# Scaling of the query rows on ScalarE instead of GpSimd, and the 32-wide products of the block inverse issued in turn for both halves

## The chip, the core and the metric

The kernel runs on one core of one Trainium2 chip. A core has TensorE (PE in the profile, matrix products; its weight loads are shown as PEld), VectorE (DVE), ScalarE (ACT), GpSimd (POOL) and SyncE (SP, which here issues most of the DMA transfers). Each engine works off its own list of instructions in order and waits for others by semaphores. The metric is the device time of one execution in microseconds (us), and the median of the runs counts.

## What is computed

The reference is one block of a hybrid sequence model, with 512 positions of width 1024 in f32: a SwiGLU feed-forward network, a mixer and a second feed-forward network, each with a residual sum and an adaptive norm. The mixer has two groups of four heads side by side, a gated delta rule and a latent attention (MLA). Cut to the parts that the change touches:

```python
# gated delta rule: a unit lower triangular system per chunk and head
M = A + jnp.eye(CHUNK, dtype=A.dtype)
W = lax.linalg.triangular_solve(M, rhs, left_side=True, lower=True, unit_diagonal=True)
...
# latent attention: the RMS norm of each head's query, plain and rotary part
q_nope = _rms(q_nope, qkn_q_nope) * scale
q_rope = _rope(_rms(q_rope, qkn_q_rope), cos[:, :, None], sin[:, :, None]) * scale
...
mixed = jnp.concatenate([o_a, o_b], axis=-1)
return mixed @ w_out
```

## The kernel before

The 512 positions are four token blocks of 128. Dense products are made in units of 128 output columns: a weight load from DRAM (tile `wr`, 512 KB, issued by SyncE at line 118), a cast to a high part on ScalarE (`wh`, line 193), the rest on VectorE (`wl`, line 198), and three matmuls of 512 columns per step of 128 (lines 266, 267 and 268) into an accumulator `pa`. There are three such PSUM buffers, and five of the other kind, `pb`, for everything small.

The code is written as generators, one per chain of small work: the delta rule, its block inverse, the preparation of queries and keys, the attention of one token block. The mixer's dense units call a step function that advances these chains at fixed rates, so that small work goes in between the 512-column matmuls of `w_in` (four groups of four units). A scheduler of the tile framework then settles the order of each engine's instructions before the run: tiles are handed out from pools, and an instruction that writes a buffer waits for the last reader of the tile that had it. A changed instruction in one chain can therefore move instructions of others, weight loads among them. After that the order is fixed.

*Queries.* `prep_q` (line 1730) takes eight tiles `upo` (four token blocks, two pairs of heads), each with two heads of 128 plain and 64 rotary columns. It works out 16 reciprocal norms for the plain part (`rqn`) and 16 for the rotary part. VectorE multiplies the rotary columns (`qrx`, by the helper `mul`, line 1206), rotates them (lines 1830 to 1834, result `qro`), and TensorE transposes `qro` at line 1768, copied to `qrT` by ScalarE at line 1770. The plain columns are multiplied in place by GpSimd, eight instructions of 128x256 (lines 1773 to 1776, by `mul`, so that the profile shows line 1206), and TensorE transposes them at line 1725.

*Block inverse.* `inverse` (line 1533) inverts, for one token block `p` and four heads at once, unit triangular blocks of 128 by doubling: the inverses of the 16-wide diagonal blocks come from `base_blocks` (forward substitution on VectorE in `bw` and `bt`, with two passes through DRAM, `a_d` to `ba` at line 1508 and `t_d` to `t` at lines 1526 and 1528), products with masks give those of 32 (lines 1553 and 1559), then of 64 (lines 1569 and 1577), then of 128 (lines 1592 and 1598). The 32-wide products use a 32x32 tile of the array each. There are two halves of the 128 rows, `j` = 0 and 64; for each half there are four products (one per head) and then a copy of the half, on ScalarE at line 1571 (`Y`), or on VectorE at line 1579 (`U`). Four inverses, one per token block, run in turn. A product in f32 issues two matmul instructions.

*Attention.* `attend` multiplies queries and keys (lines 1847 and 1850), takes row maxima on VectorE (`mx`, line 1856), exponentials on ScalarE (line 168, `pr`), transposes (line 1867), copies (`pT`, line 1871), multiplies with the values (line 1877) and copies the result (`ao`, line 1879). `attended` norms it (`on`), transposes it (line 1900) and splits it (`mh`, line 1905, on ScalarE; `ml`, line 1906, on VectorE). In the same stretch ScalarE copies the finished gate units `z` out of their accumulators (line 1921).

Of the kernel before, what the change touches and what calls it, by code (L numbers as in the profile page):

```python
# [14 lines left out]
AF = mybir.ActivationFunctionType  # L15
# [3 lines left out]
P = 128  # L19
# [60 lines left out]
class Block:  # L80
# [1452 lines left out]
    def inverse(self, p):  # L1533

        nc = self.nc
        h4 = lambda x: x.rearrange("p (h d) -> p h d", h=4)
        hs = lambda h: slice(h * P, (h + 1) * P)
        at = self.at[p]

        def flip(src):  # L1540

            t = self.slot(s="T")
            nc.vector.transpose(out=t, in_=src)
            return t

        t = self.slot(s="t0")
        self.mul(t.rearrange("p (h i c) -> p h i c", h=4, i=8),
                 self.t16[:, 4 * p:4 * p + 4, :].unsqueeze(2).to_broadcast([P, 4, 8, 16]),
                 self.dmask.rearrange("p (i c) -> p i c", i=8).unsqueeze(1).to_broadcast([P, 4, 8, 16]))
        u = flip(t)  # L1550
        py = self.aux()
        for h in range(4):
            nc.tensor.matmul(py[:, hs(h)], at[:, hs(h)], t[:, hs(h)], start=True, stop=True)
        y = self.slot(s="Y")
        self.mul(h4(y), h4(py), self.lmask.unsqueeze(1).to_broadcast([P, 4, P]))
        yield
        pz = self.aux()
        for h in range(4):
            nc.tensor.matmul(pz[:, hs(h)], y[:, hs(h)], u[:, hs(h)], start=True, stop=True)
        un = self.slot(s="U")  # L1560
        nc.vector.tensor_tensor(out=un, in0=u, in1=pz, op=ALU.subtract)
        t = flip(un)
        yield

        py, y = self.aux(), self.slot(s="Y")
        for j in (0, 64):
            a, b = slice(j, j + 32), slice(j + 32, j + 64)
            for h in range(4):
                nc.tensor.matmul(py[b, 32 * h:32 * h + 32], at[a, h * P + j + 32:h * P + j + 64],
                                 t[a, h * P + j:h * P + j + 32], start=True, stop=True, tile_position=(j, j + 32))  # L1570
            nc.scalar.copy(y[b, :P], py[b, :P])
        yield
        pz = self.aux()
        for j in (0, 64):
            a, b = slice(j, j + 32), slice(j + 32, j + 64)
            for h in range(4):
                nc.tensor.matmul(pz[a, 32 * h:32 * h + 32], y[b, 32 * h:32 * h + 32],
                                 un[b, h * P + j + 32:h * P + j + 64], start=True, stop=True, tile_position=(j + 32, j))
            nc.vector.tensor_scalar(out=h4(un[a, :])[:, :, j + 32:j + 64],
                                    in0=pz[a, :P].rearrange("p (h c) -> p h c", h=4), scalar1=-1.0, scalar2=None,  # L1580
                                    op0=ALU.mult)
        yield

        a, b = slice(0, 64), slice(64, P)
        pt, t = self.aux(), self.slot(s="T")
        for h in range(4):
            nc.tensor.transpose(pt[a, 64 * h:64 * h + 64], un[a, h * P:h * P + 64], self.ident[a, a])
        nc.scalar.copy(t[a, :256], pt[a, :256])
        yield
        py, y = self.aux(), self.slot(s="Y")  # L1590
        for h in range(4):
            nc.tensor.matmul(py[b, 64 * h:64 * h + 64], at[a, h * P + 64:h * P + P], t[a, 64 * h:64 * h + 64], start=True,
                             stop=True, tile_position=(0, 64))
        nc.scalar.copy(y[b, :256], py[b, :256])
        yield
        pz = self.aux()
        for h in range(4):
            nc.tensor.matmul(pz[a, 64 * h:64 * h + 64], y[b, 64 * h:64 * h + 64], un[b, h * P + 64:h * P + P], start=True,
                             stop=True, tile_position=(64, 0))
        nc.vector.tensor_scalar(out=h4(un[a, :])[:, :, 64:], in0=pz[a, :256].rearrange("p (h c) -> p h c", h=4),  # L1600
                                scalar1=-1.0, scalar2=None, op0=ALU.mult)
        yield
        self.inv[p] = un
# [126 lines left out]
    def prep_q(self, q):  # L1730

        nc = self.nc

        room = self.slot(s="sq3")
        s3, ve = room[:, :48], room[:, 48:80]
        for b in range(NB):
            for g in range(2):
                c = 6 * (2 * b + g)
                s = self.slot(s="aqq")
                nc.scalar.activation(s[:, :384], q[b][g][:, :384], AF.Square)  # L1740
                nc.vector.tensor_reduce(out=s3[:, c:c + 6], in_=s[:, :384].rearrange("p (e d) -> p e d", e=6), axis=AX.X,
                                        op=ALU.add)
            if b % 2:
                yield
        s3 = s3.rearrange("p (q e) -> p q e", e=3)
        nc.vector.tensor_tensor(out=ve[:, :16], in0=s3[:, :, 0], in1=s3[:, :, 1], op=ALU.add)
        nc.vector.tensor_scalar(out=ve[:, :16], in0=ve[:, :16], scalar1=1.0 / 128, scalar2=EPS, op0=ALU.mult, op1=ALU.add)
        nc.vector.tensor_scalar(out=ve[:, 16:], in0=s3[:, :, 2], scalar1=1.0 / 64, scalar2=EPS, op0=ALU.mult, op1=ALU.add)
        r = self.rsqrt(ve, 32, room[:, 80:112], room[:, 112:144])
        rqn, rqr = r[:, :16], r[:, 16:]  # L1750

        qr = []
        for b in range(0, NB, 2):
            x = self.slot(s="qrx").rearrange("p (b h c) -> p b h c", b=2, h=4)
            for e in range(2):
                for g in range(2):
                    qv = q[b + e][g][:, :384].rearrange("p (h d) -> p h d", h=2)[:, :, 128:]
                    c = 4 * (b + e) + 2 * g
                    self.mul(x[:, e, 2 * g:2 * g + 2, :], qv, self.bc(rqr[:, c:c + 2], 2, 64))
            o = self.slot(s="qro")  # L1760
            tb = lambda t: t[:, b:b + 2, :].unsqueeze(2).to_broadcast([P, 2, 4, 64])
            self.rope(o.rearrange("p (b h c) -> p b h c", b=2, h=4), x, tb(self.rope_c["q"]), tb(self.rope_s["q"]))
            qr += [o[:, :256], o[:, 256:]]
            yield
        for g in range(2):
            pt = self.aux()
            for b in range(NB):
                nc.tensor.transpose(pt[:, b * P:(b + 1) * P], qr[b][:, g * P:(g + 1) * P], self.ident)
            t = self.slot(s="qrT")
            nc.scalar.copy(t, pt)  # L1770
            self.qrT.append(t)

        for b in range(NB):
            for g in range(2):
                qv = q[b][g][:, :384].rearrange("p (h d) -> p h d", h=2)[:, :, :128]
                self.mul(qv, qv, self.bc(rqn[:, 4 * b + 2 * g:4 * b + 2 * g + 2], 2), nc.gpsimd)
        yield
        for h in range(4):
            c = (h % 2) * 192
            self.qnT.append(self.head_tiles([q[b][h // 2][:, c:c + P] for b in range(NB)], self.gqn))  # L1780
            yield
# [324 lines left out]
```

## Time and profile before

| | before |
|---|---|
| runs | 1076.95, 1079.23 and 1079.45 us, median 1079.23 |
| the profiled execution | 1077.71 us, span from first to last instruction 1076.0 |
| mean granted clock of TensorE | 0.987 of full |
| busy: PE, DVE, ACT, POOL | 1046.7, 689.4, 445.3, 51.3 us |
| GpSimd's eight scalings (`upo`) | from 490.80, 5.62 us |
| TensorE's wait for `qro` behind them | 2.60 us, up to 497.02 |
| TensorE's longest wait inside the mixer, for `z` | 4.29 us, up to 600.61 |
| 32-wide matmuls, lines 1569 and 1577 | 64 each, 193 ns each, from 622.33 to 641.4 |

A row of a timeline gives the start in us from the span's start, the length, engine, line, operation, what it writes and reads, how many instructions are grouped (x8; their length then runs from the first start to the last end), and in brackets the idle time of the engine just before, with what ended it. A row of waits gives who waited, for whom, the sum, the number and the longest. A row of the windows gives for each engine its busy time and the instructions, then the granted clock, the share of the DMA engines and GB/s. Matmul instructions overlap, so the distance between their starts, not their length, tells the rate.

### The profile page before, as it was taken

The numbers are of one execution on the slowest core, as the hardware profiler recorded it, in microseconds if no ns is written. First come the engines' busy times: TensorE is split into PE (matmuls) and PEld (weight loads), VectorE is DVE, ScalarE is ACT, GpSimd is POOL, SyncE is SP. The second block draws the span as 40 slices with busy tenths as digits, with TensorE's granted clock in tenths as the row PEclk, the third lists the DMA queues.
The fourth block names the chain that finished last, engine by engine and source line by source line (L and its number), as shares of the span: only waits on it lengthen the run. The fifth ranks groups of instructions, "written<-read, shape, count | busy, mean of one in ns | idle before, by whom it ended". The sixth has DMA issues, their size and how long they took to land. (4 is left out here: it accounts for less than half of the span.)

```text
span 1076.0 us, 15659 instructions
## 1 busy us (share of the span) xinstructions
PE 1046.7 (97%) x6183; PEld 899.1 (84%) x6183; DVE 689.4 (64%) x1231; ACT 445.3 (41%) x761; POOL 51.3 (5%) x103
## 2 busy tenths in 40 slices
PE   6999999999999999998999899999999999999998
PEld 5788878788887898887778578988899999999997
DVE  4488983433577445558868644769768787777633
ACT  3342222222222245566575363465534444444322
POOL 1000000000000011102000030220000000000000
PEclk8999999999999999999999898999999999999999
DMA  9989963233698349411203001153432333233222
GB/s 274 277 240 310 301 203 99 81 98 93 199 289 263 95 120 240 113 49 40 79 25 92 26 21 39 40 126 91 129 107 79 118 115 98 83 118 99 67 71 79
DMA packets 203687, 136.85 MB, mean 127 GB/s; under 512 B 13777, under 2 KB 186590, under 8 KB 203614
## 3 DMA queue, kind: packets, MB, share of 16 engines
q1 hardware_dynamic: 202318, 131.14, 41.1%
q0 software_dynamic: 1296, 4.72, 2.4%
q8 instruction: 48, 0.79, 0.3%
q14 instruction: 25, 0.20, 0.1%
HBM read 128.63 MB, written 2.49 MB: 122 GB/s over the span
## 5 line engine op out<-in xcount | busy, mean ns | idle before, releaser
L266 PE MATMUL pa<-hh,wh 128*128 128x512 f32 (+1 forms) x597 | 227.0, 380 | 4.3 <-ACT z L1921 4.3
L268 PE MATMUL pa<-hh,wl 128*128 128x512 f32 (+1 forms) x597 | 225.0, 377 | 2.7 <-DMA wl<-wr 2.7
L267 PE MATMUL pa<-hl,wh 128*128 128x512 f32 (+1 forms) x597 | 224.8, 377 | 0.0
L193 ACT CAST wh<-wr 128x1024 fp32r<-128x1024 f32 (+1 forms) x106 | 108.0, 1019 | 258.3 <-PE pa L267 184.4
L198 DVE TENSOR_TENSOR wl<-wr,wh 128x1024 fp32r<-128x1024 f32 (+1 forms) x97 | 114.4, 1180 | 99.0 <-ACT wh L193 94.5
L266 PE MATMUL pa<-ah,wh 128*128 128x512 f32 (+1 forms) x396 | 145.5, 367 | 0.6 <-DVE xT L873 0.4
L267 PE MATMUL pa<-al,wh 128*128 128x512 f32 (+1 forms) x396 | 144.5, 365 | 0.0
L268 PE MATMUL pa<-ah,wl 128*128 128x512 f32 (+1 forms) x396 | 143.5, 362 | 0.0
L266 PEld LDWEIGHTS pa<-hh,wh 128*128 128x128 f32 x597 | 113.6, 190 | 27.2 <-ACT z L1921 4.7
L268 PEld LDWEIGHTS pa<-hh,wl 128*128 128x128 f32 x597 | 113.5, 190 | 23.1 <-DMA wl<-wr 3.3
L267 PEld LDWEIGHTS pa<-hl,wh 128*128 128x128 f32 x597 | 113.5, 190 | 19.2 <-DVE hl L453 0.4
L268 PEld LDWEIGHTS pa<-ah,wl 128*128 128x128 f32 x396 | 74.8, 189 | 12.0
L266 PEld LDWEIGHTS pa<-ah,wh 128*128 128x128 f32 x396 | 75.2, 190 | 10.4 <-ACT wh L193 1.7
L267 PEld LDWEIGHTS pa<-al,wh 128*128 128x128 f32 x396 | 75.2, 190 | 7.2
L551 DVE SCALAR_TENSOR_TENSOR aa<-ar,sc,aa 128x512 f32<-128x512 f32 x98 | 73.2, 751 | 9.7 <-DMA ar<-in_w_ada 8.5
L846 PE MATMUL pb<-fh,wh 128*128 128x256 f32 x144 | 40.7, 282 | 0.0
L848 PE MATMUL pb<-fh,wl 128*128 128x256 f32 x144 | 40.7, 283 | 0.0
L848 PE MATMUL pb<-hh,wl 128*128 128x256 f32 x144 | 40.7, 283 | 0.0
L847 PE MATMUL pb<-fl,wh 128*128 128x256 f32 x144 | 40.7, 282 | 0.0
L847 PE MATMUL pb<-hl,wh 128*128 128x256 f32 x144 | 40.7, 282 | 0.0
L846 PE MATMUL pb<-hh,wh 128*128 128x256 f32 x144 | 40.6, 282 | 0.0
L873 DVE SCALAR_TENSOR_TENSOR xT<-pa,mod,xT 128x512 f32<-128x512 f32 (+1 forms) x40 | 29.4, 736 | 17.5 <-PE pa L268 17.5
(433 smaller groups left out, 1995.0 us busy)
## 6 DMA issues: line engine op xcount, KB each, us to landing
wr<-in_ffn_w_in SPq DMA_DIRECT2D x82, 512.0 KB, 4.1
ar<-in_w_ada SPq DMA_DIRECT2D x48, 512.0 KB, 5.9
wr<-in_ffn_w_out SPq DMA_DIRECT2D x34, 512.0 KB, 3.4
ar<-in_w_ada SPq DMA_DIRECT2D x48, 256.0 KB, 4.8
wr<-in_w_in SPq DMA_DIRECT2D x21, 512.0 KB, 3.9
wr<-in_ffn_w_out SPq DMA_DIRECT2D x17, 384.0 KB, 3.4
wl<-wr POOLq DMA_DIRECT2D x9, 512.0 KB, 5.6
wr<-in_w_out SPq DMA_DIRECT2D x8, 512.0 KB, 4.8
```

The source lines that it names most:

```text
L193: self.nc.scalar.copy(hi, raw)
L198: self.nc.vector.tensor_tensor(out=lo, in0=raw, in1=hi.bitcast(F32), op=ALU.subtract)
L266: mm(out, wh, xh, start=start, stop=False)
L267: mm(out, wh, xl, start=False, stop=False)
L268: mm(out, wl, xh, start=False, stop=stop)
L551: nc.vector.scalar_tensor_tensor(out=acc, in0=a, scalar=sc, in1=acc, op0=ALU.mult, op1=ALU.add)
L846: mm(out, wh, xh, start=start and k == 0, stop=False, **kw)
L847: mm(out, wh, xl, start=False, stop=False, **kw)
L848: mm(out, wl, xh, start=False, stop=stop and k == 3, **kw)
L873: nc.vector.scalar_tensor_tensor(out=self.xT[t][:, ts], in0=p[:, ts], scalar=gate[:, t:t + 1], in1=self.xT[t][:, ts], op0=ALU.mult, op1=AL ...
```

## The change

The first part replaces GpSimd's eight multiplications of 128x256 by sixteen activations of 128x128 on ScalarE, each with a scale per row. The second turns the two loops of the 32-wide products around: the heads are now the outer loop and the halves the inner one, and the two copies follow when all eight products are issued. Tiles, sizes and numbers of products stay.

```diff
         py, y = self.aux(), self.slot(s="Y")
-        for j in (0, 64):
-            a, b = slice(j, j + 32), slice(j + 32, j + 64)
-            for h in range(4):
+        for h in range(4):
+            for j in (0, 64):
+                a, b = slice(j, j + 32), slice(j + 32, j + 64)
                 nc.tensor.matmul(py[b, 32 * h:32 * h + 32], at[a, h * P + j + 32:h * P + j + 64],
                                  t[a, h * P + j:h * P + j + 32], start=True, stop=True, tile_position=(j, j + 32))
+        for j in (0, 64):
+            b = slice(j + 32, j + 64)
             nc.scalar.copy(y[b, :P], py[b, :P])
         yield
         pz = self.aux()
-        for j in (0, 64):
-            a, b = slice(j, j + 32), slice(j + 32, j + 64)
-            for h in range(4):
+        for h in range(4):
+            for j in (0, 64):
+                a, b = slice(j, j + 32), slice(j + 32, j + 64)
                 nc.tensor.matmul(pz[a, 32 * h:32 * h + 32], y[b, 32 * h:32 * h + 32],
                                  un[b, h * P + j + 32:h * P + j + 64], start=True, stop=True, tile_position=(j + 32, j))
+        for j in (0, 64):
+            a = slice(j, j + 32)
             nc.vector.tensor_scalar(out=h4(un[a, :])[:, :, j + 32:j + 64],
...
         for b in range(NB):
             for g in range(2):
-                qv = q[b][g][:, :384].rearrange("p (h d) -> p h d", h=2)[:, :, :128]
-                self.mul(qv, qv, self.bc(rqn[:, 4 * b + 2 * g:4 * b + 2 * g + 2], 2), nc.gpsimd)
+                for e in range(2):
+                    qv, c = q[b][g][:, 192 * e:192 * e + P], 4 * b + 2 * g + e
+                    nc.scalar.activation(qv, qv, AF.Copy, scale=rqn[:, c:c + 1])
```

In the lists of the new kernel, tiles from about number 4314 on have numbers higher by 8, and lines lie lower: 1770 is 1774, 1847 is 1852, 1850 is 1855, 1877 is 1882, 1900 is 1905, and the new scaling is line 1781.

*The first place: ScalarE at the scaling.* Before, ScalarE goes there from the values (`vn`) over silu of a convolution (`cv`) and the copies of the delta rule's Gram block (`l2q`, `ktk`) to a weight cast (`wh`):

```order
L1320 ACTIVATE vn_4041<-pa_4205,ry_3787 128x256
L168 ACTIVATE cv_4200<-cv_4200 128x512
L1430 ACTIVATE l2q_4269<-pb_4264 128x512
L1433 COPY ktk_4271<-pb_4264 128x512
L193 CAST wh_4625<-wr_4624 128x1024
L1410 ACTIVATE cv_4361<-pa_4224,cwT_808 128x512
```

In the new kernel the scalings stand in between:

```order
L1781 ACTIVATE upo_3832<-upo_3832,sq_4094 128x128 x2
L1781 ACTIVATE upo_3916<-upo_3916,sq_4094 128x128
L168 ACTIVATE cv_4200<-cv_4200 128x512
L1781 ACTIVATE upo_3916<-upo_3916,sq_4094 128x128
L1781 ACTIVATE upo_3850<-upo_3850,sq_4094 128x128 x2
L1781 ACTIVATE upo_3934<-upo_3934,sq_4094 128x128 x2
L1430 ACTIVATE l2q_4269<-pb_4264 128x512
L1433 COPY ktk_4271<-pb_4264 128x512
L1781 ACTIVATE upo_3868<-upo_3868,sq_4094 128x128 x2
L1781 ACTIVATE upo_3952<-upo_3952,sq_4094 128x128 x2
L1781 ACTIVATE upo_3886<-upo_3886,sq_4094 128x128 x2
L1781 ACTIVATE upo_3970<-upo_3970,sq_4094 128x128 x2
```

Eight of the sixteen stand ahead of the copy to `l2q`, eight between that of `ktk` and the cast.

*The second place: TensorE ahead of its wait for `z`.* `pa_5349` is the last gate unit but one, and `pa_5471` (`pa_5479` in the new kernel) the next, which takes a buffer that `z`'s copy frees. Before:

```order
L266 MATMUL pa_5349<-hh_3169,wh_5227 128x512
L1900 MATMUL pb_5182<-ident_92,on_5180 128x128 x4
L1553 MATMUL pb_5197<-t_5193,at_4551 128x128 x4
L1847 MATMUL pb_5204<-nT_4530,nT_4359 128x256
L1847 MATMUL pb_5205<-nT_4543,nT_4384 128x256
L1850 MATMUL pb_5204<-krT_4426,qrT_4298 128x256
L1850 MATMUL pb_5205<-krT_4426,qrT_4298 128x256
L267 MATMUL pa_5349<-hl_3170,wh_5227 128x512
L268 MATMUL pa_5349<-hh_3169,wl_5228 128x512
L266 MATMUL pa_5471<-hh_3155,wh_5344 128x512
```

and in the new kernel:

```order
L266 MATMUL pa_5357<-hh_3169,wh_5235 128x512
L267 MATMUL pa_5357<-hl_3170,wh_5235 128x512
L268 MATMUL pa_5357<-hh_3169,wl_5236 128x512
L1905 MATMUL pb_5190<-ident_92,on_5188 128x128 x4
L1553 MATMUL pb_5205<-t_5201,at_4559 128x128 x4
L1852 MATMUL pb_5212<-nT_4538,nT_4367 128x256
L1852 MATMUL pb_5213<-nT_4551,nT_4392 128x256
L1855 MATMUL pb_5212<-krT_4434,qrT_4298 128x256
L1855 MATMUL pb_5213<-krT_4434,qrT_4298 128x256
L266 MATMUL pa_5479<-hh_3155,wh_5352 128x512
```

The unit's last two matmuls have moved ahead of the transposes of `on`, the first block product and the attention's products. SyncE's list (weight loads `wr`, the two passes through DRAM) before:

```order
L1504 DMA a_d<-bd_4879 128x16x32
L1508 DMA ba_4897<-a_d 64x16x16 x2
L118 DMA wr_5737<-in_w_out 128x4x256
L118 DMA wr_5882<-in_w_out 128x4x256
L118 DMA wr_6003<-in_w_out 128x4x256
L1526 DMA t_d<-bt_4900 64x256 x2
L1528 DMA t_5138<-t_d 128x16x16
L118 DMA wr_6121<-in_w_out 128x4x256
```

and in the new kernel:

```order
L1504 DMA a_d<-bd_4887 128x16x32
L118 DMA wr_5745<-in_w_out 128x4x256
L1508 DMA ba_4905<-a_d 64x16x16 x2
L118 DMA wr_5890<-in_w_out 128x4x256
L118 DMA wr_6011<-in_w_out 128x4x256
L1526 DMA t_d<-bt_4908 64x256 x2
L118 DMA wr_6129<-in_w_out 128x4x256
L1528 DMA t_5146<-t_d 128x16x16
```

Each of the two reads back from DRAM has got a weight load ahead of it.

*The third place: the 32-wide products on TensorE.* `pb_5440` and `pb_5478` hold the products of the first two inverses; the other rows are gate matmuls and the attention's. Before (a row counts products, each of which issues two matmuls):

```order
L1569 MATMUL pb_5440<-T_5333,at_4551 32x32 x4
L267 MATMUL pa_5471<-hl_3164,wh_5344 128x512
L1877 MATMUL pb_5452<-vn_4038,pT_5406 128x128
...
L1569 MATMUL pb_5478<-T_5363,at_4552 32x32 x4
L268 MATMUL pa_5471<-hh_3163,wl_5345 128x512
L266 MATMUL pa_5471<-hh_3165,wh_5344 128x512
L1569 MATMUL pb_5440<-T_5333,at_4551 32x32 x4
L1877 MATMUL pb_5452<-vn_4038,pT_5432 128x128
...
L1569 MATMUL pb_5478<-T_5363,at_4552 32x32 x4
```

and in the new kernel:

```order
L1569 MATMUL pb_5448<-T_5341,at_4559 32x32 x8
L267 MATMUL pa_5479<-hl_3164,wh_5352 128x512
L1882 MATMUL pb_5460<-vn_4038,pT_5414 128x128
...
L1569 MATMUL pb_5486<-T_5371,at_4560 32x32 x8
L268 MATMUL pa_5479<-hh_3163,wl_5353 128x512
L266 MATMUL pa_5479<-hh_3165,wh_5352 128x512
L267 MATMUL pa_5479<-hl_3166,wh_5352 128x512
```

All eight products of a token block stand in one row, where they were two rows of four with other work between them.

## The prediction

> **What bounds the kernel now.** I read the busy times of the page first, then TensorE's list of waits, then the timelines around the changed lines. Every row is of the one profiled execution, 1077.71 us long with a span of 1076.0; the page opens so:
>
> ```profile
> span 1076.0 us, 15659 instructions
> PE 1046.7 (97%) x6183; PEld 899.1 (84%) x6183; DVE 689.4 (64%) x1231; ACT 445.3 (41%) x761; POOL 51.3 (5%) x103
> ```
>
> TensorE (PE) works in 97% of the span and sets the end: an edit counts by what it takes out of TensorE's row, or by a wait that it shortens there. TensorE's waits, longest in total first:
>
> ```profile
> PE pa L266 <- ACT z L1921: 4.3, 1, 4.3
> ...
> PE pb L1768 <- DVE qro L1834: 2.8, 2, 2.6
> ```
>
> The second row is the end of the chain through the query scaling; the first lies among the instructions that the new order moves. The three stretches follow in the order of the program.
>
> **1. The scaling leaves GpSimd (POOL): -2.6 us.** POOL, VectorE (DVE), then TensorE, start and length ahead of each row:
>
> ```profile
> 490.80 5.62 POOL L1206 TENSOR_TENSOR upo<-upo,sq 128x256 f32<-128x256 f32 x8 [23.95 <-DVE sq L189]
> ```
> ```profile
> 491.25 2.17 DVE L1206 TENSOR_TENSOR qrx<-upo,sq 128x128 f32<-128x128 f32 x4
> ...
> 495.98 0.98 DVE L1834 TENSOR_TENSOR qro<-rt,rt 128x512 f32<-128x512 f32 x1
> ...
> 497.48 0.89 DVE L1206 TENSOR_TENSOR qrx<-upo,sq 128x128 f32<-128x128 f32 x4
> ...
> 499.87 0.69 DVE L1834 TENSOR_TENSOR qro<-rt,rt 128x512 f32<-128x512 f32 x1
> ```
> ```profile
> 494.03 0.39 PE L267 MATMUL pa<-hl,wh 128*128 128x512 f32 x1
> 497.02 0.66 PE L1768 MATMUL pb<-ident,qro 128*128 128x128 f32 x4 [2.60 <-DVE qro L1834]
> ```
>
> VectorE makes qro (the rotated queries) once beside POOL's eight instructions and once after them. Beside them the group takes 496.96 - 491.25 = 5.71 us; after them 500.56 - 497.48 = 3.08 us. Nothing else differs between the two groups, so the scaling slows VectorE by 2.63 us, and TensorE waits 2.60 us for that very product. With POOL still, qro is ready near 491.25 + 3.08 = 494.33, as TensorE gets there (its 512-column matmuls start 0.23 us apart): the wait of 2.60 goes. The waits row has 0.2 at the second group, which I leave.
>
> ScalarE (ACT) gets 16 instructions of 128x128 in place of POOL's 8 of 128x256. No row shows this form from SBUF to SBUF; nearest are two of 128x128 and, for room, what stands next on ScalarE:
>
> ```profile
> L1879 ACT COPY ao<-pb 128x128 f32<-128x128 f32 x16 | 4.1, 266 | 6.3 <-PE pb L1877 6.1
> L1660 ACT ACTIVATE o<-pb,eG 128x128 f32<-128x128 f32 x12 | 3.4, 370 | 4.7 <-PE pb L1658 4.7
> ```
> ```profile
> 499.28 1.05 ACT L193 CAST wh<-wr 128x1024 fp32r<-128x1024 f32 x1 [5.59 <-PE pa L267]
> ```
>
> By those, 16 x 0.27 to 0.37 = 4.3 to 5.9 us, and I take 4.3 (a plain copy with a scale). ScalarE is idle for 5.59 us ahead of that cast, and the eight new instructions that stand ahead of the copies of l2q and ktk delay only VectorE's row sums. So they are costed at nothing; cover gone, the last scaled tiles come up to 0.9 us late for TensorE's transposes of the queries (L1725). Could ScalarE slow VectorE as POOL did? A gain of nothing is the lower bound there, 2.6 the upper. I take the upper: the second group of VectorE ran beside ScalarE's cast and was the fast one.
>
> **2. The long wait at 596 us: -1.5 us.** The new order changes what stands around it on TensorE, ScalarE, VectorE and the queue of SyncE (SP):
>
> ```profile
> 592.42 0.63 PE L1900 MATMUL pb<-ident,on 128*128 128x128 f32 x4 [0.87 <-DVE on L1206]
> 593.03 1.13 PE L1553 MATMUL pb<-t,at 128*128 128x128 f32 x8
> ...
> 594.95 0.70 PE L1850 MATMUL pb<-krT,qrT 64*128 64x256 f32 x4
> 595.59 0.50 PE L267 MATMUL pa<-hl,wh 128*128 128x512 f32 x1
> ...
> 600.61 0.80 PE L266 MATMUL pa<-hh,wh 128*128 128x512 f32 x1 [4.29 <-ACT z L1921]
> ```
> ```profile
> 596.12 1.05 ACT L193 CAST wh<-wr 128x1024 fp32r<-128x1024 f32 x1 [6.80 <-PE pa L267]
> ...
> 598.48 0.47 ACT L168 ACTIVATE pr<-pb,mx 128x256 f32<-128x256 f32 x1
> ...
> 599.97 0.59 ACT L1921 COPY z<-pa 128x512 f32<-128x512 f32 x1
> ```
> ```profile
> 592.19 0.69 DVE L1206 TENSOR_TENSOR t<-t,mk 128x512 f32<-128x512 f32 x1
> ...
> 595.88 0.42 DVE L1856 TENSOR_REDUCE mx<-pb 128x1 f32<-128x256 f32 x1
> ```
> ```profile
> 588.01 0.37 SPq L1528 DMA_DIRECT2D t<-t_d  x1
> 588.47 0.97 SPq L118 DMA_DIRECT2D wr<-in_w_out  x1
> ```
>
> TensorE's matmul at 600.61 writes a buffer that z's copy still reads. z stands on ScalarE behind the cast, which waits 6.80 us for the matmul of line 267 at 595.59, and behind the exponentials. In the new order lines 267 and 268 stand ahead of the transposes of line 1900: the cast is released at about 591.9, and no longer sits between the first row maximum (ready 595.88 + 0.42 = 596.30) and the first exponential (598.48). From there to the end of z's copy are 600.56 - 598.48 = 2.08 us, so z would be done near 598.4.
>
> Against this, on SyncE the two loads of ba, and later the load of t (the inverses of the 16-wide diagonal blocks, which line 1553 multiplies), now each stand behind a 512-KB weight load. The DMA page of 560 to 596 us gives moved GB/s by 0.9-us slices and the landing times:
>
> ```profile
> GB/s 0 0 0 0 79 145 67 0 7 102 205 387 27 0 0 0 0 18 0 0 0 0 0 0 23 269 300 207 311 124 77 0 64 107 258 269 30 0 0 0
> ...
> wr<-in_w_out SPq DMA_DIRECT2D x4, 512.0 KB, 4.8
> ...
> ba<-a_d SPq DMA_DIRECT2D x2, 64.0 KB, 2.7
> ```
>
> At the fastest slice, 387 GB/s, 512 KB pass in 1.35 us (estimate); I take 1.4 for ba and 0.6 more for t, since most of its weight load passes while SyncE still waits for t_d. Both bounds: 0, or the full landing of 4.8. t landed at about 588.01 + 2.7 = 590.7, 1.5 us ahead of VectorE's use of it at 592.19. Landing 2.0 later, it holds line 1553 back by 0.5, and z ends at 598.9 in place of 600.56: 1.7 us less wait, of which I take 1.5, because the second maximum may hold the second exponential. Bounds: the whole 4.29 gained; or t 4.8 later, z at 598.4 + 4.8 - 1.5 = 601.7, and 1.1 us lost.
>
> **3. The products of 32 in turn: -0.7 us.** Their matmuls, and a place where row halves already alternate (lines 1592 and 1598, at a granted clock of 0.50, below):
>
> ```profile
> 624.85 0.40 PE L266 MATMUL pa<-hh,wh 128*128 128x512 f32 x1
> 625.18 0.43 PE L1569 MATMUL pb<-T,at 32*32 32x32 f32 x8
> 625.54 1.16 PE L1877 MATMUL pb<-vn,pT 128*128 128x128 f32 x8
> ...
> 636.54 0.66 PE L1900 MATMUL pb<-ident,on 128*128 128x128 f32 x4 [0.56 <-DVE on L1206]
> 637.13 1.52 PE L1577 MATMUL pb<-U,Y 32*32 32x32 f32 x48
> ...
> 646.06 0.31 PE L1592 MATMUL pb<-T,at 64*64 64x64 f32 x1
> 646.12 0.31 PE L1598 MATMUL pb<-U,Y 64*64 64x64 f32 x1
> ```
>
> The count of matmuls stays (64 each; a product issues two). In a run of 48 they start about 0.03 us apart. A burst of 8 costs more: 0.33 us from the 512-column matmul ahead where 0.23 is usual, and 0.36 to the next instruction where 8 x 0.03 = 0.24 would do: 0.22 us a burst. Line 1569 has seven bursts before and three in the new order, line 1577 three and one: six fewer, 6 x 0.22 = 1.3. Some of it runs into waits that another engine ends (0.56 at 636.54), so I take half, 0.7.
>
> Does alternating also run the halves side by side? At 646.06 alternating instructions start 0.06 apart at half clock, 0.03 at full: the rate that the 32-wide ones already have. I count nothing; bounds 0 and 128 x 0.015 = 1.9, if the interval halved. The Trainium skill speaks for that bound: "TensorE: Matmul & The Clock Gate", in the table that advises on small-K and small-M matmuls, has tiles in distinct row groups start within 4 ns of each other; by that figure every second instruction gains 0.026 us, and the sum would be an estimated 64 x 0.026 = 1.7 us lower. No row of before shows it.
>
> **Sum.** -2.6 - 1.5 - 0.7 = -4.8: the profiled 1077.71 becomes 1072.9. The median of before, 1079.23, lies 1.5 above the profiled time, and to it the same sum gives **1074.4**. A measurement can tell about 0.3%, 3.2 us: under 1076.0 is faster.
>
> **The rivals.**
>
> *Given back, no change (0.28).* The lower ends meet: ScalarE's instructions delay the queries (0.9), ba's delay goes down the whole VectorE chain so that the wait at 596 stays 4.29, and bursts only move waits. -2.6 + 0.9 = -1.7: 1077.5. For it: TensorE has no other slack, so each lateness shows in full. Against: the cast's move takes 2.2 us out of the chain to z.
>
> *The clock stays up, faster still (0.12).* The clock by 40 slices of 26.9 us on the page, and by windows of 2 us (third number from the end):
>
> ```profile
> PEclk8999999999999999999999898999999999999999
> ```
> ```profile
> 598.00:600.00 2.00, 0.00 (x0) 0.00 (x0) 0.42 (x1) 1.99 (x7) 0.00 (x0) 0.66 0.19 25
> 600.00:602.00 2.00, 1.39 (x4) 0.98 (x5) 1.85 (x3) 0.56 (x2) 0.00 (x0) 0.50 0.68 237
> ...
> 604.00:606.00 2.00, 2.00 (x10) 1.68 (x9) 1.63 (x3) 0.59 (x1) 0.00 (x0) 0.63 0.00 0
> ```
>
> After the 4.29 us of idleness TensorE works at 0.50 from 600.6 until about 605.5 (0.63 over the last window is 1.48 us at half and 0.52 at full), which costs half of 4.9, 2.4 us. If a wait of 2.8 no longer lowers the clock: -7.2, 1072.0. For it: the slice with the 2.60 us at 494, the 19th, has a 9 like its neighbours. The Trainium skill, same page, Part 1, has the clock fall after an idle window of about 3.4 us whose phase is free; by it a wait of 2.8 would be too short. The trace agrees only in part, since the fall at about 598.6 came 2.3 us into the idleness.
>
> *Turns in one bank cost, slower (0.12).* Both halves write one PSUM tile, and in turn the row group changes at each product. If an instruction may not enter until one of the other row group has left, each change costs its length less the usual interval. The group of 48 above has 0.19 us instructions: 0.19 - 0.03 = 0.16, for 64 changes 10.2 us. Without term 3: -4.1 + 10.2 = +6.1, 1085.3; from 0.11 us a change it is beyond 0.3% of slower. For it: no row of before alternates row groups in one bank. Against: lines 1592 and 1598 alternate at no cost, though in two buffers. The Trainium skill speaks for it: "TensorEngine Tiling (Array Packing)", Restrictions and Gotchas, says that different row tiles cannot access the same PSUM bank simultaneously. No run here shows what that does.
>
> **How the numbers follow.** The forecast has 0.48. The rivals have 0.28, 0.12 and 0.12. Faster by over 0.3% is 0.48 + 0.12 = 0.60, less 0.01 for forecast cases that end just above 1076.0: 0.59; within 0.3%: 0.29; slower: 0.12. The range goes from 1070.5 (the clock's case with part of the side-by-side bound) to 1079.0 (the returned gain, 1077.5, with 1.5 for the spread of the runs of before); the slower case, 0.12, and some 0.05 below lie outside.
>
> **What would show it.** Right: qro's first group takes about 3.1 us, TensorE's wait at line 1768 is under 0.5; z's wait is 2 to 3.5; 32-wide matmuls stand 0.03 apart in three bursts and one. Wrong: VectorE still slow beside ScalarE's scaling; a new wait for upo, t or Y on TensorE over 1 us; 32-wide matmuls 0.1 us or more apart; z's wait still above 4.

## The result

The changed kernel takes 1070.51 us (median of 11 runs, 1067.26 to 1077.72), the kernel before 1078.77 (11 runs, 1076.64 to 1082.87): a ratio of 0.9938, interval 0.9918 to 0.9958, faster by 0.6%. The forecast was 1074.4. The profiled execution took 1070.54 us:

```profile
span 1068.8 us, 15669 instructions
PE 1039.9 (97%) x6183; PEld 893.8 (84%) x6183; DVE 687.3 (64%) x1231; ACT 448.3 (42%) x777; POOL 45.6 (4%) x95
```

The runs of the changed kernel are not one heap. Each run comes with its mean granted TensorE clock:

| granted clock | changed kernel, us | before, us |
|---|---|---|
| 0.997 to 0.994 | 1067.3 to 1068.7 (4 runs) | 1072.1 (one of 80) |
| 0.992, 0.991 | 1070.5 (3 runs) | 1072.7 to 1074.2 (3 of 80) |
| 0.987, 0.986 | 1076.7 to 1077.2 (3 runs) | 1076.9 to 1080.8 (32 of 80) |
| 0.984 | 1077.7 (1 run) | 1079.6 to 1082.2 (14 of 80) |

(The 80 runs of before are those that ran beside the experiments.) At an equal clock the changed kernel is ahead by 2 to 4 us. The rest of the 8.3 us is that its runs get a higher clock more often. A straight line through 198 runs of twelve series (one slope for all, one offset for each kernel) has 0.91 us for each 0.001 of clock and a residual of 0.8 us. It is an estimate: it takes a thousandth of the mean clock to cost the same wherever in the run it is lost. By it the changed kernel, with 12 more runs from below, has **3.0 +- 0.4 us less at equal clock**; its mean clock of 0.9897 against 0.9867 is worth another 3.0 x 0.91 = 2.7. Together that is the difference of the means, 1078.6 - 1072.8 = 5.8, to within 0.1; the median says 8.3 because it falls into the upper group of clocks.

### The profile page after: what moved, and what is told of

Read it like the earlier page. It is cut to its first block, busy times and chain, and to the rows that moved or that the text cites. A ratio compares the mean times of both kernels' runs of the same rounds, so it can differ in the third digit from the quotient of the medians.

```text
span 1068.8 us, 15669 instructions
## 1 busy us (share of the span) xinstructions
PE 1039.9 (97%) x6183; PEld 893.8 (84%) x6183; DVE 687.3 (64%) x1231; ACT 448.3 (42%) x777; POOL 45.6 (4%) x95
## 4 chain that ended last, share of the span: by engine, by line
PE 85%; DVE 5%; ACT 4%; DMA 3%; issue 2%; POOL 1%; SPq 0%; POOLq 0%; DVEq 0%; ACTq 0%
PE pa L266 19%; PE pa L267 19%; PE pa L268 19%; PE pb L847 5%; PE pb L846 5%; PE pb L848 5%; DMA wl<-wr 1%; PE pb L1852 1%; PE pb L414 1%; PE pb L267 1%; PE pb L268 1%; PE pb L266 1%; PE pb L1468 1%; DVE wl L198 1%; PE pb L1855 1%
```

## The profile after

*The scaling.* TensorE's waits of the changed kernel have no row for qro any more:

```profile
PE pa L266 <- ACT z L1926: 4.1, 1, 4.1
...
PE pb L1905 <- DVE on L1206: 3.2, 3, 1.6
...
PE pb L1553 <- DVE t L1206: 1.3, 1, 1.3
```

VectorE's first group of rotary queries, and TensorE around their transposes:

```profile
492.67 0.89 DVE L1206 TENSOR_TENSOR qrx<-upo,sq 128x128 f32<-128x128 f32 x4
...
494.98 0.69 DVE L1839 TENSOR_TENSOR qro<-rt,rt 128x512 f32<-128x512 f32 x1
```
```profile
495.51 0.39 PE L267 MATMUL pa<-hl,wh 128*128 128x512 f32 x1
495.74 0.65 PE L1772 MATMUL pb<-ident,qro 128*128 128x128 f32 x4
```

The group takes 495.67 - 492.67 = 3.00 us where it took 5.71, and the transposes start 0.23 us behind the matmul ahead of them.

*The wait for z.* TensorE, ScalarE and VectorE there:

```profile
590.90 0.63 PE L1905 MATMUL pb<-ident,on 128*128 128x128 f32 x4 [0.44 <-DVE on L1206]
592.84 1.13 PE L1553 MATMUL pb<-t,at 128*128 128x128 f32 x8 [1.31 <-DVE t L1206]
...
599.61 0.80 PE L266 MATMUL pa<-hh,wh 128*128 128x512 f32 x1 [4.14 <-ACT z L1926]
```
```profile
590.26 1.05 ACT L193 CAST wh<-wr 128x1024 fp32r<-128x1024 f32 x1 [0.20 <-PE pa L267]
596.19 1.28 ACT L168 ACT_TABLE_LOAD   x1 [4.88 <-DVE mx L1861]
597.49 0.47 ACT L168 ACTIVATE pr<-pb,mx 128x256 f32<-128x256 f32 x1
...
598.97 0.59 ACT L1926 COPY z<-pa 128x512 f32<-128x512 f32 x1
```
```profile
592.00 0.69 DVE L1206 TENSOR_TENSOR t<-t,mk 128x512 f32<-128x512 f32 x1 [1.25 <-DMA t<-t_d]
...
595.69 0.42 DVE L1861 TENSOR_REDUCE mx<-pb 128x1 f32<-128x256 f32 x1
```

The cast did come early, six microseconds ahead of the exponentials. The load of ScalarE's table for the exponential did not: it starts only when the first row maximum is there (596.19), so 1.28 us stay between the two. And t lands late enough to make a new wait of 1.31. The wait for z is 4.14 where it was 4.29. SyncE issues the load of t here:

```profile
588.11 0.37 SPq L1528 DMA_DIRECT2D t<-t_d  x1
```

That is no earlier than before (588.01), though TensorE has its transposes of line 1900 (now 1905) 1.52 us earlier; so a good part of the lateness is there before the load is issued. The size of the new wait isn't fixed either: a second profile of the same kernel (the series under "Once more" below) has 0.77 for t, with 0.45 for `on` ahead of it and 4.15 for z.

*The products of 32.* All of them in the changed kernel, with the transposes ahead of two:

```profile
621.91 0.44 PE L1569 MATMUL pb<-T,at 32*32 32x32 f32 x16
...
623.74 0.44 PE L1569 MATMUL pb<-T,at 32*32 32x32 f32 x16
...
629.17 0.63 PE L1905 MATMUL pb<-ident,on 128*128 128x128 f32 x4 [1.14 <-DVE on L1206]
629.72 0.69 PE L1569 MATMUL pb<-T,at 32*32 32x32 f32 x32
...
635.80 0.63 PE L1905 MATMUL pb<-ident,on 128*128 128x128 f32 x4 [1.63 <-DVE on L1206]
636.36 1.20 PE L1579 MATMUL pb<-U,Y 32*32 32x32 f32 x64
```

Sixteen now take 0.44 us, eight took 0.43: start to start (1.20 - 0.19) / 63 = 0.016 us. From each start to that of the next instruction, all 128 take 2.58 us where they took 4.98: 2.40 less. But the three waits for the normed attention rows (`on`) sum to 0.44 + 1.14 + 1.63 = 3.21, where the waits row of before has 1.8:

```profile
PE pb L1900 <- DVE on L1206: 1.8, 3, 0.9
```

The first is shorter (0.44 for 0.87); the other two, beside the products, are 2.77 where they were 1.8 - 0.87 = 0.9: `on` comes from ScalarE, VectorE and GpSimd in turn, which got no faster, and 1.8 us go back there.

*The clock.* Windows of before at the first (TensorE busy time ahead, the clock third from the end), then of the changed kernel:

```profile
644.00:648.00 4.00, 4.00 (x36) 3.44 (x35) 0.45 (x2) 2.09 (x4) 0.00 (x0) 0.50 0.00 0
```
```profile
600.00:604.00 4.00, 4.00 (x16) 3.50 (x16) 2.51 (x5) 0.52 (x1) 0.00 (x0) 0.50 0.00 0
...
644.00:648.00 4.00, 4.00 (x45) 3.62 (x44) 3.34 (x7) 0.92 (x1) 0.00 (x0) 1.00 0.00 0
```

The half clock behind the wait for z is still there. The one over the small products, from 643.0 to 653.3 us in the profile of before, is not in this profile. From 622 to the transposes behind the small products the changed kernel gains 5.0 us: its first product starts 0.42 us earlier (621.91 for 622.33), the transposes of line 1420 behind the last start 5.4 us earlier (647.31 for 652.71). Most of that is the clock: 10.2 us at half clock cost up to 5.1 us (estimate: half of them).

## The experiments

Beside each stands its time at equal clock against before, by the line above (+- is the 95% interval of that fit), an estimate of what the program does by itself; the median has the clocks in it.

**One part alone: the scaling.** The last part of the change, with the two product loops of before.

```diff
-                self.mul(qv, qv, self.bc(rqn[...], 2), nc.gpsimd)
...
+                    nc.scalar.activation(qv, qv, AF.Copy, scale=rqn[:, c:c + 1])
```

> Only the scaling on ScalarE; the 32-wide products as before. The new order of the changed kernel (weight load ahead of the block inverses' loads, last unit ahead of the transposes) comes with this part. Theory (program time from three places, the rest of the 8.3 us from the granted clock): the wait for qro (2.60 us) is gone, the wait for z stays near 4.1, 32-wide matmuls stay 0.03 us apart, and the time lies about 2.6 us under before at the same lost clock, near 1076 us. Rival (the gain is made in the scaling and in the order that comes with it): most of the 8.3 us is here, near 1071 us.

Median 1074.68 us (12 runs), ratio 0.9966 (0.9946 to 0.9986); at equal clock -2.3 +- 0.5. The wait for qro is gone, z's wait is 4.15, and a new one of 1.00 for t is there: the order of the second place comes with the scaling. The theory's 2.6 lies inside the interval; the rival's 1071 does not hold.

**The other part alone: the products in turn.**

> Only the products in turn; the scaling on GpSimd as before, and SyncE's order as before. Theory: 32-wide matmuls 0.016 us apart, some 2.4 us out of TensorE's row, about 1 of it given back in waits for the normed attention rows, and the runs fall into groups by granted clock: those without half clock in the 64-wide products some 5 us or more under before, the others 1 to 2.5 under. Rival (all of it is program time): every run 5 to 6 us under before, at the same granted clock as before.

Median 1069.37 us (6 runs), ratio 0.9926 (0.9903 to 0.9950); at equal clock -0.7 +- 0.7. The wait for qro is back with 2.60, the waits for `on` sum to 3.6. Four of the six runs have a clock of 0.997, which none of the 80 runs of before reached, so the rival fails; the theory's 2.4 less 1 is more than the 0.7 found. So the part that does least at equal clock moves the median most.

**The products grouped, not in turn.** As few bursts, halves one after the other, both copies behind:

```diff
-        for h in range(4):
-            for j in (0, 64):
+        for j in (0, 64):
+            for h in range(4):
...
```

> The changed kernel, but with the four products of one half and then the four of the other, and both copies behind all eight: as few bursts, no alternation. Theory (alternation lets the halves run side by side): 32-wide matmuls back at 0.03 us, lines of 16 take 0.65 to 0.7 us instead of 0.44, TensorE's row some 1.5 to 2 us longer than in the changed kernel. Rival (fewer bursts are the gain): same as the changed kernel within 0.5 us of program time, 16 matmuls in 0.44 us.

Median 1076.03 us (12 runs), ratio 0.9961 (0.9940 to 0.9983); at equal clock -2.5 +- 0.5. Its products:

```profile
621.10 0.59 PE L1569 MATMUL pb<-T,at 32*32 32x32 f32 x16
...
635.67 1.51 PE L1579 MATMUL pb<-U,Y 32*32 32x32 f32 x64
```

Both were half right. Sixteen take 0.59, between the 0.44 in turn and the 0.65 expected. By length, the products of the grouped kernel sum to 0.59 + 0.59 + 0.89 + 1.51 = 3.58 and of the changed one to 0.44 + 0.44 + 0.69 + 1.20 = 2.77: alternation is worth 0.8 us of the 2.4, and the bursts the other 1.6. At equal clock it lies 0.5 +- 0.6 behind the changed kernel. Its mean clock, 0.9880, is near that of the scaling alone (0.9888), but so is that of the changed kernel's second series below (0.9888).

**GpSimd busy at the same time.** The changed kernel, and beside ScalarE's scaling:

```diff
...
+                o2 = one.rearrange("p (h d) -> p h d", h=2)
+                self.mul(o2, o2, self.bc(rqn[:, 4 * b + 2 * g:4 * b + 2 * g + 2], 2), nc.gpsimd)
```

> The changed kernel, and GpSimd multiplies a tile of its own eight times by the same norms at the same time, 128x256 each; nobody reads the result. Theory (GpSimd slows VectorE): the first group of the rotary queries takes about 5.7 us again instead of 3.0, the second 3.1, and TensorE waits about 2 us for qro. Rival (VectorE was slow because it read the tiles that GpSimd was writing): 3.0 us and no wait.

One run, 1078.57 us; by the line it is 3.3 +- 1.6 behind the changed kernel. GpSimd, VectorE and TensorE:

```profile
489.58 6.36 POOL L1206 TENSOR_TENSOR one<-one,sq 128x256 f32<-128x256 f32 x8 [23.86 <-DVE sq L189]
```
```profile
490.11 1.75 DVE L1206 TENSOR_TENSOR qrx<-upo,sq 128x128 f32<-128x128 f32 x4
...
494.49 0.98 DVE L1843 TENSOR_TENSOR qro<-rt,rt 128x512 f32<-128x512 f32 x1
```
```profile
495.53 0.66 PE L1774 MATMUL pb<-ident,qro 128*128 128x128 f32 x4 [2.19 <-DVE qro L1843]
```

VectorE's group takes 495.47 - 490.11 = 5.36 us again, though GpSimd touches none of its tiles but the norms, which both read. The norms aren't it: `qro` is made of two tiles `rt` that GpSimd never touches, and takes 0.98 as before the change, for 0.69 in the changed kernel. What slowed VectorE is that GpSimd multiplies beside it, and the wait of 2.19 follows. Its run also has half clock over the small products (17 us from 637.3, by windows of 1 us), with the same instructions there as the changed kernel, whose profile has none.

**The array kept busy in the small products.** The changed kernel with an idle product ahead of each block's products at three stages, overwritten by them:

```diff
         pz = self.aux()
+        nc.tensor.matmul(pz[:, :256], at[:, :P], at[:, :256], start=True, stop=True)
...
```

> The changed kernel with twelve idle products of 128x128 by 128x256 added, one ahead of each block's products at lines 1579, 1596 and 1602 (their result is overwritten), about 0.48 us each, 5.8 us of TensorE's row in all. Theory (the half clock around 637 to 655 us comes from windows in which the small products leave the array mostly idle): the half clock there is gone from nearly every run, no run has a granted clock under 0.988, and the time is some 5.8 us over the fast runs of the changed kernel, 1073 to 1076 us, in one narrow group. Rival (the half clock comes at random, whatever TensorE does there): a third of the runs still at 0.987 and below, those near 1082 us.

Median 1077.13 us (12 runs, 1074.71 to 1079.38); at equal clock +4.8 +- 0.6 against before, so 7.8 over the changed kernel: more than the 5.8 for the idle products. Its trace has most of the surplus: from its start to that of the products behind it an idle product takes 0.52 to 0.63 us and not 0.48, the twelve 7.2 in all. No run is under 0.990, where 9 of 23 runs of the changed kernel and 59 of 80 of before are at 0.988 or under. So the half clock depends on what TensorE does in that stretch; that it is the one over the small products which is gone from all twelve follows only from their mean clocks, since one run was profiled.

**t and ba past the weight loads.**

```diff
-            nc.sync.dma_start(a[64 * e:64 * e + 64, :].rearrange("p (s c) -> p s c", s=16),
+            nc.gpsimd.dma_start(a[64 * e:64 * e + 64, :].rearrange("p (s c) -> p s c", s=16),
...
-        nc.sync.dma_start(self.t16, t_d.rearrange("q i s c -> (i s) q c"))
+        nc.gpsimd.dma_start(self.t16, t_d.rearrange("q i s c -> (i s) q c"))
```

> The changed kernel with the loads of ba and of t issued on GpSimd's queue, so that no weight load stands ahead of them. Theory (the weight load ahead of t cost 1.3 us of new wait and cancelled the gain at z): TensorE's wait for t at line 1553 goes from 1.3 to under 0.3 us, the copy of z comes about 1.3 us earlier, the wait for z stays about 4, and the gap from the transposes of the normed attention rows to the next unit is about 1.3 us shorter. Rival (t is late for other reasons, GpSimd's queue or VectorE's chain): the wait at line 1553 stays above 1 us.

Median 1069.51 us (6 runs); at equal clock -2.4 +- 0.7, no better than the changed kernel. GpSimd's row:

```profile
591.22 1.20 POOL L1528 DMA_DIRECT2D t<-t_d  x1 [15.51 <-PE pb L1882]
592.51 1.03 POOL L179 TENSOR_TENSOR ry<-ve,mhalf 128x4 f32<-128x4 f32 x1
```

The wait for t is 0.78, short of the 0.3 expected, and no better than the 0.77 that the changed kernel has in its second profile. From issue to landing t takes 3.7 us here, 3.9 and 3.4 in the two profiles of the changed kernel, so taking it off SyncE's queue did not make it faster. The load takes 1.20 us of GpSimd's list, and the reciprocal norm (`ry`) that `on` needs stands behind it: the waits for `on` are 3.6. So the theory isn't borne out, and what the weight load alone costs stays open.

**z on VectorE.**

```diff
-            nc.scalar.copy(z, p)
+            nc.vector.tensor_copy(out=z, in_=p)
```

> The changed kernel with the four copies of z on VectorE in place of ScalarE. Theory (TensorE waits for z only because z stands behind the table load and the exponentials on ScalarE): z is copied right behind the second row maximum, near 597 us, the wait goes from 4.1 to about 1.9 us, and with the shorter idleness the half clock after it is gone in part of the runs; 2 us less at the same clock. Rival (the wait moves to the next reader of the exponentials, the transposes of pr): the wait for z is short, and TensorE waits as long at line 1872.

Median 1070.36 us (12 runs); at equal clock -1.8 +- 0.5, worse than the changed kernel. VectorE there:

```profile
597.94 0.75 DVE L1911 SCALAR_TENSOR_TENSOR ml<-pb,cwT,mh 128x512 fp32r<-128x512 f32 x1 [2.43 <-ACT mh L1910]
598.61 0.68 DVE L1926 COPY z<-pa 128x512 f32<-128x512 f32 x1
```

Neither theory nor rival: z stands behind `ml`, `ml` waits for `mh`, and `mh` stands behind the exponentials on ScalarE. The wait for z grew to 5.06. Both edits together:

> Both edits together: ba and t on GpSimd's queue, z on VectorE. Theory: both gains add, 3 to 3.5 us of program time under the changed kernel, and no half clock at 600 us in most runs. Rival: the waits give way to that for pr, and the sum is no better than the better of the two.

Median 1073.44 us (12 runs); at equal clock -1.4 +- 0.5. The gains did not add, since neither was one.

**The table early.**

```diff
+        if (i, g) == (1, 1):
+            self.table(self.dume, self.ident[:, 0:1], AF.Exp)
         ps = [self.aux() for _ in heads]
...
```

> The changed kernel with one exponential of a single column ahead of the attention's second block of the second pair of heads, so that the table is loaded before the row maxima come. Theory (the table load of 1.28 us, which waits for the first row maximum, is what kept the wait for z as long as before): no table load between the row maximum and the exponential, the wait for z falls from 4.1 to about 2.9 us, 1.3 us of program time. Rival (the wait is set elsewhere): the exponentials come earlier, and the wait for z stays above 3.8.

ScalarE, then TensorE:

```profile
592.95 0.47 ACT L168 ACTIVATE pr<-pb,mx 128x256 f32<-128x256 f32 x1 [4.75 <-DVE mx L1863]
```
```profile
595.14 0.50 PE L266 MATMUL pa<-hh,wh 128*128 128x512 f32 x1 [2.93 <-ACT z L1928]
```

The exponential starts as soon as the maximum is there, and the wait for z is 2.93, as the theory had it. Median 1072.06 us (11 runs, 1066.64 to 1076.94), ratio 0.9935 (0.9909 to 0.9962); at equal clock -4.1 +- 0.5 against before, 1.0 +- 0.6 less than the changed kernel. At equal clock it is the best program of the study, and its lowest run is the lowest of all; only two of its 11 runs are at 0.991 and above. This profile has no half clock behind the wait, where every other one has; it does have 17 us of it over the small products.

**Once more, on one chip with the last.**

> The changed kernel once more, for the mixture of granted clocks beside the next kernel and the kernel before on one chip. Theory (2.8 us of program time, the rest by the clock): at a given granted clock 2 to 3.5 us under before; a part of the runs at 0.991 and above, where before has a few in a hundred. Rival (the clocks of the first runs were chance): the same mixture as before, and the median 2 to 3.5 us under before's.

Median 1073.95 us (12 runs), ratio 0.9954 (0.9926 to 0.9983); at equal clock -3.1 +- 0.5. Five of the 12 runs are at 0.991 and above (with the first series 12 of 23; of before 4 of 80), five at 0.988 and under.

> Only the products in turn, once more, with more runs. Theory (the turn shortens the stretch of small products, and with it the chance that a clock window falls into idle array): more than half of the runs at 0.990 and above, and the median 5 us or more under before, with only 0.5 to 1.5 us of it at equal clock. Rival: the mixture of before.

Median 1072.13 us (12 runs), ratio 0.9943 (0.9917 to 0.9968); at equal clock -0.4 +- 0.5. Nine of 12 runs at 0.991 and above, with the first series 14 of 18, one at 0.988 or under. The theory's mixture holds; at equal clock it is at the lower edge of what was expected.

## Why the prediction was right, and where it was not

*The sum's size for the program was too large: 4.8 forecast, 3.0 +- 0.4 at equal clock. The clock, forecast as a rival of 0.12, made up for it.* That the number came out near is in part luck: of the 5.8 us between the means 2.7 are clock, which the sum of 4.8 did not have. The range, 1070.5 to 1079.0, holds the median of 1070.51 by a hundredth; the second series of the same kernel has 1073.95, close to the forecast's 1074.4. And two of the signs of being wrong that the prediction named did come: z's wait above 4 (4.14), and a new wait for t over 1 us (1.31, in one of two profiles). Point by point:

- **The scaling, -2.6: right.** The group of rotary queries went from 5.71 to 3.00 us, the wait from 2.60 to nothing. Alone it is worth 2.3 +- 0.5. The cause, GpSimd's work beside VectorE's, is shown by the run that puts GpSimd's work back. ScalarE's sixteen instructions take 5.0 us where 4.3 was taken, and cost TensorE no more than a small split of the transposes of line 1729.
- **The wait for z, -1.5: wrong, 0.15, and with the new wait for t a loss.** The step that failed: "From there to the end of z's copy are 600.56 - 598.48 = 2.08 us, so z would be done near 598.4". It took the exponential to start at the row maximum, with the table load out of the way like the cast. The load stands behind the same wait for the maximum (4.88 us idle, then 1.28). The run with the table early shows it: 2.93. The second step, that t comes 0.5 late to line 1553, was too small: 1.31, while the transposes ahead of it came earlier by 0.43 us less wait. 1.31 - 0.43 - 0.15 = 0.7 us lost where 1.5 was to be won; by the second profile, 0.77 - 0.42 - 0.14, it is 0.2. The step took 2.7 us for t to land, but that row of the DMA page is `ba`'s: the profile of before has no landing of t, and in the changed kernel it takes 3.9 and 3.4.
- **The products, -0.7: right in sign, made of other terms.** The bursts are worth 1.6, not 1.3, and alternating does run the halves side by side, which was counted at nothing with a bound of 1.9: 0.8. The step that failed compared 0.06 us at half clock with 0.03 at full and took that for a floor; the floor is 0.016 or less. It set 64-wide products in turn beside 32-wide ones of one half. The profile of before has the like to compare, right behind the rows in turn and at the same half clock:

```profile
646.33 3.30 PE L1598 MATMUL pb<-U,Y 64*64 64x64 f32 x29
```

These 29 of one half start (3.30 - 0.31) / 28 = 0.107 us apart, the ones in turn 0.06: in turn the halves already ran side by side, and a row of before did show it. Of the 2.4 us the waits for `on` took back 1.8, more than the half that was set aside. That leaves 0.6; alone the turn is worth 0.5 +- 0.5 at equal clock (18 runs).

- **Turns in one bank cost: refuted.** Products of two row groups write one tile in turn, and 16 take as long as 8 did. The Trainium skill, "TensorEngine Tiling (Array Packing)", Restrictions and Gotchas, says that different row tiles cannot access the same PSUM bank simultaneously; that cost no time here, where the halves write other partitions. The Trainium skill, "TensorE: Matmul & The Clock Gate", in its table with small-K matmuls, has tiles in distinct row groups start at most 4 ns apart; here that is not reached, 16 ns on average.
- **The clock: right that it could rise, wrong about where.** The wait of 4.14 still lowers it at 600 us. What fell away is the half clock over the small products at 640: both profiles of the changed kernel (mean clocks 0.992 and 0.993) lack it, and its runs at 0.987 and under suggest that a part of the runs still has it.

The sum of the traces: 2.6 + 2.4 - 1.8 - 0.7 = 2.5 us, 3.0 with the 0.2 of the second profile, and 0.2 for the second wait for qro, which is gone too; by the runs at equal clock 3.0 +- 0.4.

*What stays open.* That the turn raises the clock is shown (14 of 18 runs at 0.991 and above, 4 of 80 before), and the run with the idle products speaks for busy work in the stretch keeping it up. Why the turn does it was only argued: fewer windows fall wholly into sparse work. The grouped products have 3 of 12 such runs, but the kernel with the table early, whose products are in turn, has only 2 of 11; series of this length don't tell the two apart. Where in a run the windows lie was not steered. That the two parts together have fewer such runs (12 of 23) than the turn alone isn't explained.

## What to carry to other kernels

Ask of each instruction that is moved out of a chain what stands behind the same semaphore wait: a table load that follows a wait isn't early because ScalarE is idle. A product that TensorE finishes sooner is a gain only as far as its next operand comes sooner too. And where the runs of one kernel spread by 1%, compare at equal granted clock before believing a median: here the part that saves 0.5 us moved it by 7 to 10.

## What the runs showed of the hardware

- VectorE's products and sums of two tiles took 1.4 to 2.1 times as long while GpSimd multiplied a tile of its own (0.98 for 0.69 us, 1.75 for 0.89, 1.58 for 0.75), and not while ScalarE did the scaling.
- Matmuls of 32x32 in two row and column groups in turn started 0.016 us apart, in one group 0.03.
- Half clock comes in stretches of 3.4, 6.8, 10.2 and 17.1 us (worked out from windows of 1 us in every profile), close to multiples of 3.41. The Trainium skill, "TensorE: Matmul & The Clock Gate", Part 1, has a free-running window of 3413 ns; the traces agree. There the Trainium skill has half clock after an idle window; here the clock also fell with TensorE busy by the profile, over small products. Before, TensorE's busy time (the number behind a window's length) is full in each of the windows ahead of the fall at 643.0:

```profile
639.00:640.00 1.00, 1.00 (x11) 0.58 (x9) 0.79 (x4) 0.14 (x2) 1.00 (x2) 1.00 0.07 16
640.00:641.00 1.00, 1.00 (x13) 0.62 (x10) 0.05 (x1) 0.56 (x2) 1.00 (x2) 1.00 0.00 0
641.00:642.00 1.00, 1.00 (x18) 0.85 (x18) 0.53 (x2) 0.23 (x1) 0.38 (x1) 1.00 0.00 0
642.00:643.00 1.00, 1.00 (x10) 0.69 (x11) 0.00 (x0) 0.78 (x3) 0.00 (x0) 1.00 0.00 0
643.00:644.00 1.00, 1.00 (x11) 1.00 (x12) 0.75 (x1) 0.00 (x0) 0.00 (x0) 0.51 0.00 0
```

- The same program took 1067.3 to 1079.7 us (23 runs of the changed kernel), the less the higher its mean clock. Its two profiles fit that: 17.0 us at half clock in the one of 1070.54 us, 13.6 in the one of 1068.80, beside 1.8 behind TensorE's last instruction.
